# A 1-core two-block transformer kernel: all weight remainders and all vector work on VectorE, the 512-column products of a group ahead of its 256-column ones, and a new start-up sequence

## The chip, the cores and the metric

The kernel runs on one core of a Trainium2 chip. The metric is the device time of one execution in microseconds (us); the median of three executions before the change is 1955.4 us.

## What is computed

Two blocks, each of two layers, run one behind the other on one sequence of 256 tokens of width 1024, in float32. The reference, cut to what matters here:

```python
def hybrid_layer(x, p_i, ...):                       # first block, two layers
    proj = rmsnorm(x, g_pre_mix) @ w_in              # 3404 columns, split into q, k, v of A to D
    o_a = dsa_attention(rope(a_q), rope(a_k), a_v, rope(a_iq), rope(a_ik), iw)   # top 64 keys by an index score
    o_b = forgetting_attention(b_q, b_k, b_v, log_sigmoid(b_f + b_forget))
    o_c = differential_attention(rope(c_q), rope(c_k), c_v, lam, lam_init, diff_subln)
    o_d = sliding_window_sink_attention(rope(d_q), rope(d_k), d_v, sinks)
    x = x + rmsnorm(concat(o_a, o_b, o_c, o_d) @ w_out, g_post_mix)
    m = square(relu(rmsnorm(x, g_pre_mlp) @ w_up)) @ w_down
    x = x + rmsnorm(m, g_post_mlp)
    return x + sigmoid(x @ w_ple_gate) * (p_i @ w_ple_proj)

def second_block(x, ...):                            # two layers
    mix = hybrid_mixer(x, ...)                       # dilated window attention, retention, gates
    x = layer_norm(ALPHA * x + mix, ln1_g, ln1_b)
    x = layer_norm(ALPHA * x + swiglu(x, ...), ln2_g, ln2_b)
```

## The kernel before

**Products of split numbers.** Every large matmul is made of three products of parts. An operand is split into `hi`, a rounded copy, and `lo`, the rest that the rounding left. For weights, `Weights.load` (lines 91 to 121) brings a tile of up to 128x1024 numbers from HBM over SP's queue into `wraw` (4 buffers, line 98), copies it on ScalarE into `whi` (6 buffers, line 104) and subtracts into `wlo` (6 buffers, line 107). Which engine subtracts is taken from a list, `lo_engines` or `next`: VectorE mostly, GpSimd for 24 of the 628 tiles. These 24 are 11 in each layer of the first block (three in turn with VectorE, then all eight of the column groups 2120 and 1608 of `w_in`) and one in each layer of the second. Activations are split in the same way into `phl` (lines 232 and 233).

**The four kinds of product.** `mm_tok` (line 270) and `mm_pair` (line 286) hold the activation still and move 512 columns of weight. `mm_dim` (lines 315 to 317) moves 256 columns. `mm_wide` holds a 128x128 piece of weight still: the product with `whi` moves both parts of the activation, 512 columns (line 328), the product with `wlo` moves the `hi` part alone, 256 columns (line 329). It runs one group of eight such pairs for each block of 128 outputs, 2080 pairs in all, in the MLPs of the first block and in the projections and gated MLPs of the second.

**A layer of the first block.** `layer1` projects column groups of `w_in` in the order 768, 1280, 0, 512, 2120, 1608, 2380, 2892 (`proj`). The first two give the queries and keys of the index. `index` adds up scores (VectorE, line 526) and takes the best 64 by eight rounds of maximum and replacement (lines 532 and 533), then makes the mask (lines 536 and 537). Meanwhile TensorE runs the projections that follow, then attention A needs the mask: its first masked logits are written by VectorE at line 388, between the matmuls of lines 387, 412 and 420. While A's short matmuls wait for VectorE and ScalarE, TensorE fills the time with matmuls of group 1608. The bq and bk transposes (lines 372 and 363) come after that. After `w_out`, `norm(t)` scales and adds the residual in `xg` (line 805) and transposes it as input of the MLP, and `update(t)` (lines 813 and 814) brings X up to date on GpSimd.

**The second block** ends its first half with a layer norm, whose last operation is line 1056 and is followed by the transposes for the gated MLP. At that place GpSimd makes one `wlo` tile.

**The start.** `begin` (line 962) loads ident, positions, the rope frequencies and eight small constants over GpSimd's queue, x over SP's, and the first norm weight as two broadcasts to 128 partitions over ScalarE's queue. VectorE multiplies x by it (line 995) before the transposes. `setup1` computes the rope tables on VectorE and ScalarE, `scale` multiplies them by each token's norm, and the rope of the first projection (line 488) waits for them.

**What sets the order.** A scheduler orders the instructions of each engine from the program; an instruction passed to `pin` keeps its place in program order, and one passed to `behind` is issued after another one of its engine. So work that is moved to another engine changes the place of its neighbours too.

## Time and profile before

| | |
|---|---|
| median of three runs | 1955.4 us (1955.16 to 1962.62) |
| the profiled execution, its own time | 1958.0 us |
| its span | 1956.1 us |
| TensorE busy | 96% of the span |
| VectorE, ScalarE, GpSimd busy | 68%, 53%, 9% |
| mean granted TensorE clock | 0.988 of full speed |

The span reaches from the first to the last instruction of the profiled execution. A busy share counts an instruction from its start to its modelled end, so TensorE's 96% holds time in which a matmul waits its turn behind another one. Rows of the timeline carry, in brackets, how long the engine was idle before and what it waited for.

### The profile page before, as it was taken

The numbers are of one execution on the slowest core, as the hardware profiler recorded it, in microseconds if no ns is written. First come the engines' busy times: TensorE is split into PE (matmuls) and PEld (weight loads), VectorE is DVE, ScalarE is ACT, GpSimd is POOL, SyncE is SP. The second block draws the span as 40 slices with busy tenths as digits, with TensorE's granted clock in tenths as the row PEclk, the third lists the DMA queues.
The fourth block names the chain that finished last, engine by engine and source line by source line (L and its number), as shares of the span: only waits on it lengthen the run. The fifth ranks groups of instructions, "written<-read, shape, count | busy, mean of one in ns | idle before, by whom it ended". The sixth has DMA issues, their size and how long they took to land. (4 is left out here: it accounts for less than half of the span.)

```text
span 1956.1 us, 27859 instructions
## 1 busy us (share of the span) xinstructions
PE 1884.0 (96%) x10280; PEld 1614.1 (83%) x10280; DVE 1320.7 (68%) x2413; ACT 1044.4 (53%) x1751; POOL 166.4 (9%) x168
## 2 busy tenths in 40 slices
PE   6998999999989999999999999999999999999997
PEld 4786878878868888988888988888897888988886
DVE  6866756677677666758666677566668666677565
ACT  4555545465645445565555555554565555555552
POOL 3302100013030000000000000000000000000000
PEclk9998999999989999999999999999999999999999
DMA  6532576645326655645555756664554555656662
GB/s 190 154 118 83 184 236 206 201 138 162 117 73 206 201 174 165 194 147 181 159 178 178 227 174 204 181 199 147 163 171 151 179 179 171 206 168 205 191 192 89
DMA packets 187208, 334.52 MB, mean 171 GB/s; under 512 B 11548, under 2 KB 108882, under 8 KB 186688
## 3 DMA queue, kind: packets, MB, share of 16 engines
q1 hardware_dynamic: 180160, 308.94, 50.2%
q0 software_dynamic: 6624, 23.27, 3.8%
q8 instruction: 81, 1.33, 0.3%
q10 hardware_dynamic: 288, 0.52, 0.1%
q14 instruction: 55, 0.45, 0.1%
HBM read 331.62 MB, written 4.62 MB: 172 GB/s over the span
## 5 line engine op out<-in xcount | busy, mean ns | idle before, releaser
L107 DVE TENSOR_TENSOR wlo<-wraw,whi 128x1024 fp32r<-128x1024 f32 (+1 forms) x604 | 694.5, 1165 | 332.8 <-ACT whi L104 319.0
L104 ACT ACTIVATE whi<-wraw 128x1024 fp32r<-128x1024 f32 (+1 forms) x628 | 615.0, 998 | 370.1 <-PE bank L286 109.4
L328 PE MATMUL bank<-phl,whi 128*128 128x512 f32 x2080 | 740.1, 399 | 0.0
L329 PE MATMUL bank<-phl,wlo 128*128 128x256 f32 x2080 | 585.1, 281 | 0.7 <-DVE wlo L107 0.7
L328 PEld LDWEIGHTS bank<-phl,whi 128*128 128x128 f32 x2080 | 390.6, 188 | 92.8 <-DVE phl L233 0.6
L329 PEld LDWEIGHTS bank<-phl,wlo 128*128 128x128 f32 x2080 | 393.0, 189 | 3.9 <-DVE wlo L107 2.5
L286 PE MATMUL bank<-whi,phl 128*128 128x512 f32 x1280 | 360.0, 396 | 1.2 <-ACT phl L232 1.0
L270 PE MATMUL bank<-whi,phl 128*128 128x512 f32 (+4 forms) x1152 | 350.1, 384 | 6.1 <-ACT whi L104 4.1
L286 PEld LDWEIGHTS bank<-whi,phl 128*128 128x128 f32 x1280 | 237.9, 189 | 54.0 <-ACT phl L232 2.9
L270 PEld LDWEIGHTS bank<-whi,phl 128*128 128x128 f32 x1152 | 214.5, 194 | 38.0 <-ACT whi L104 5.2
L270 PE MATMUL bank<-wlo,phl 128*128 128x512 f32 (+4 forms) x576 | 216.3, 376 | 0.5 <-DVE wlo L107 0.5
L286 PE MATMUL bank<-wlo,phl 128*128 128x512 f32 x640 | 206.3, 394 | 0.1
L286 PEld LDWEIGHTS bank<-wlo,phl 128*128 128x128 f32 x640 | 120.5, 188 | 29.1 <-DVE wlo L107 2.4
L227 POOL TENSOR_TENSOR ry<-ry,mhalf 128x1 f32<-128x1 f32 (+1 forms) x40 | 33.0, 827 | 1152.8 <-DVE ry L226 1145.5
L270 PEld LDWEIGHTS bank<-wlo,phl 128*128 128x128 f32 x576 | 111.2, 193 | 16.0 <-DVE wlo L107 1.7
L317 PE MATMUL bank<-phl,wlo 128*128 128x256 f32 x304 | 86.5, 285 | 0.0
L316 PE MATMUL bank<-phl,whi 128*128 128x256 f32 x304 | 86.3, 284 | 0.0
L315 PE MATMUL bank<-phl,whi 128*128 128x256 f32 x304 | 85.5, 281 | 0.0
L232 ACT ACTIVATE phl<-bank 128x512 fp32r<-128x512 f32 (+2 forms) x64 | 35.3, 573 | 53.9 <-PE bank L251 53.2
L315 PEld LDWEIGHTS bank<-phl,whi 128*128 128x128 f32 x304 | 57.8, 190 | 0.6
L317 PEld LDWEIGHTS bank<-phl,wlo 128*128 128x128 f32 x304 | 57.6, 189 | 0.0
L233 DVE TENSOR_TENSOR phl<-bank,phl 128x512 fp32r<-128x512 f32 (+2 forms) x64 | 41.0, 661 | 24.5 <-ACT phl L232 24.4
(297 smaller groups left out, 1838.0 us busy)
## 6 DMA issues: line engine op xcount, KB each, us to landing
wraw<-in_w_in_dram SPq DMA_DIRECT2D x172, 512.0 KB, 4.5
wraw<-in_w_mlp_up_dram SPq DMA_DIRECT2D x64, 512.0 KB, 4.6
wraw<-in_w_mlp_down_dram SPq DMA_DIRECT2D x64, 512.0 KB, 4.5
wraw<-in_w_ffn_gate_dram SPq DMA_DIRECT2D x44, 512.0 KB, 4.6
wraw<-in_w_ffn_up_dram SPq DMA_DIRECT2D x44, 512.0 KB, 4.4
wraw<-in_w_ffn_down_dram SPq DMA_DIRECT2D x44, 512.0 KB, 4.5
wraw<-in_w_in_dram SPq DMA_DIRECT2D x54, 384.0 KB, 3.8
wraw<-in_w_out_dram SPq DMA_DIRECT2D x32, 512.0 KB, 3.8
```

Of the source, the lines that this page charges most:

```text
L104: nc.scalar.activation(hi[:, :n], src, AF.Copy)
L107: ins = eng.tensor_tensor(lo[:, :n], src, hi[:, :n].bitcast(F32), op=ALU.subtract)
L227: nc.gpsimd.tensor_tensor(y, y, self.mhalf[:, :n], op=ALU.pow)
L232: self.nc.scalar.activation(hi, src, AF.Copy)
L233: self.nc.vector.tensor_tensor(lo, src, hi.bitcast(F32), op=ALU.subtract)
L270: self.order(nc.tensor.matmul(ps, self.part(parts, kt)[x][:, sl], get(kt + kbase)[w], start=start and n == 0, stop=stop and n == len(terms ...
L286: ins = nc.tensor.matmul(pss[j], self.part(parts, kt)[x][:, sl], get(kt + kbase)[w][:, j * 512:(j + 1) * 512], start=start and n == 0, sto ...
L315: self.order(nc.tensor.matmul(ps, wh, xh, start=first, stop=False, **kw), n == 0)
L316: nc.tensor.matmul(ps, wh, xl, start=False, stop=False, **kw)
L317: nc.tensor.matmul(ps, wl, xh, start=False, stop=last, **kw)
L328: self.order(nc.tensor.matmul(flat, wh[:, c:c + P], both, start=n == 0, stop=False), n == 0)
L329: nc.tensor.matmul(ps[:, 0], wl[:, c:c + P], both[:, :S], start=False, stop=n == len(kts) - 1)
```

## The change

- `mm_wide` issues the eight 512-column products of a group first and the eight 256-column ones after them.
- The choice of an engine for `wlo` is gone: all 628 subtractions run on VectorE. The product of two norm weights (`gboth`), the two products `gain(t)` and the update of X, which GpSimd did, are on VectorE as well. The update reads PSUM itself, with the norm and the weight in one operation per half, so two ScalarE copies per token tile are gone; it is placed after `relu2(1)`.
- The start: the first norm weight is loaded as 8x128 numbers, transposed on TensorE into columns, and applied to the transposed x from PSUM. ident, norm weight, positions and frequencies come over ScalarE's queue. The first splits are pinned in order. The rope tables are made after x of both token tiles has been taken. The loads of the lambdas, masks and other constants stay on GpSimd's queue, behind `scale(1)`. The first projection runs on six of its eight pieces before it lets the other work in.

The core of the diff (line numbers of the changed file are 2 to 40 off those above):

```diff
@@ Weights.load
-            nc.scalar.activation(hi[:, :n], src, AF.Copy)
-            eng = self.next.pop(0) if self.next else self.lo_engines[self.n % len(self.lo_engines)]
-            self.n += 1
-            ins = eng.tensor_tensor(lo[:, :n], src, hi[:, :n].bitcast(F32), op=ALU.subtract)
+            first = nc.scalar.activation(hi[:, :n], src, AF.Copy)
+            ins = nc.vector.tensor_tensor(lo[:, :n], src, hi[:, :n].bitcast(F32), op=ALU.subtract)
@@ mm_wide
-            wh, wl = get(kt)
-            self.order(nc.tensor.matmul(flat, wh[:, c:c + P], both, start=n == 0, stop=False), n == 0)
-            nc.tensor.matmul(ps[:, 0], wl[:, c:c + P], both[:, :S], start=False, stop=n == len(kts) - 1)
+            self.order(nc.tensor.matmul(flat, get(kt)[0][:, c:c + P], both, start=n == 0, stop=False), n == 0)
+        for n, kt in enumerate(kts):
+            nc.tensor.matmul(ps[:, 0], get(kt)[1][:, c:c + P], self.part(parts, kt)[0], start=False,
+                             stop=n == len(kts) - 1)
@@ layer1
-            self.late.append(self.setup1)
-            self.late.append(lambda: scale(0))
+            self.late += [lambda: scale(0), lambda: scale(1), self.constants]
...
-        self.w.lo_engines = [nc.vector, nc.gpsimd]
         ps = proj(0, 512)
...
-        self.w.lo_engines = [nc.gpsimd]
         ps = proj(2120, 260)
...
-        nc.gpsimd.tensor_tensor(gboth, gboth, gmlp, op=ALU.mult)
+        self.pin(nc.vector.tensor_tensor(gboth, gboth, gmlp, op=ALU.mult))
...
-            nc.gpsimd.tensor_tensor(o, X[t], gmlp, op=ALU.mult)
+            nc.vector.tensor_tensor(o, X[t], gmlp, op=ALU.mult)
...
-                self.pin(nc.scalar.activation(u[:, sl], pss[t][j], AF.Copy, scale=r))
-            us[t] = u
-            self.pin(nc.gpsimd.tensor_tensor(us[t], us[t], gpost, op=ALU.mult))
-            nc.gpsimd.tensor_tensor(X[t], X[t], us[t], op=ALU.add)
+                self.pin(nc.vector.scalar_tensor_tensor(u[:, sl], pss[t][j], rs[t], gpost[:, sl], op0=ALU.mult,
+                                                        op1=ALU.mult))
+            self.pin(nc.vector.tensor_tensor(X[t], X[t], u, op=ALU.add))
@@ begin
-        nc.gpsimd.dma_start(self.ident, self.a["ident"])
...
-            nc.scalar.dma_start(g[:, sl], self.a["norm_pre_mix"][0, sl].partition_broadcast(P))
+        nc.scalar.dma_start(self.ident, self.a["ident"])
+        nc.scalar.dma_start(gr, self.a["norm_pre_mix"][0].rearrange("(k p) -> k p", p=P))
...
+        self.late += [lambda: load(1), lambda: take(1, 0), lambda: take(1, 1), self.setup1, second, lambda: squares(0),
+                      lambda: squares(1)]
@@ second block, gated MLP
-                self.w.next = [nc.vector] * 3 + [nc.gpsimd]
```

**How the order moves, 1: the remainders of groups 2120 and 1608.** GpSimd before, in the first layer, from the end of group 512 on (the numbers behind the names tell buffers apart; 780 and 260 columns are group 2120, 1024 are two pieces of group 1608):

```order
L107 TENSOR_TENSOR wlo_733<-wraw_730,whi_732 128x780
L107 TENSOR_TENSOR wlo_739<-wraw_736,whi_738 128x780
L107 TENSOR_TENSOR wlo_745<-wraw_742,whi_744 128x260
L107 TENSOR_TENSOR wlo_751<-wraw_748,whi_750 128x260
L107 TENSOR_TENSOR wlo_894<-wraw_891,whi_893 128x1024
L107 TENSOR_TENSOR wlo_900<-wraw_897,whi_899 128x1024
L107 TENSOR_TENSOR wlo_906<-wraw_903,whi_905 128x1024
L107 TENSOR_TENSOR wlo_912<-wraw_909,whi_911 128x1024
```

VectorE after the change, same layer, the end of the top-64 search, the mask, and later the first tiles of group 1608:

```order
L529 MAX top_664<-score_502 128x8
L103 TENSOR_TENSOR wlo_749<-wraw_746,whi_748 128x260
L530 MATCH_REPLACE score_502<-top_664,score_502 128x256
L103 TENSOR_TENSOR wlo_755<-wraw_752,whi_754 128x260
L533 TENSOR_SCALAR score_494<-score_494 128x128
...
L387 ISA pr_790,mx_789<-bank_791,score_494 128x128
...
L487 TENSOR_TENSOR rope_890<-bank_806,cr32_284 128x8x16
L103 TENSOR_TENSOR wlo_898<-wraw_895,whi_897 128x1024
...
L103 TENSOR_TENSOR wlo_904<-wraw_901,whi_903 128x1024
```

The last remainders of group 2120 stand at the end of the search, and the first of group 1608 stands 24 instructions behind the first masked logits, where GpSimd made it during the search.

**2: TensorE at the same place.** Before, the matmuls of group 1608 (line 270) ahead of the first of the two logits matmuls that wait for the mask (line 387):

```order
L270 MATMUL bank_915<-whi_893,phl_132 128x512
L270 MATMUL bank_915<-wlo_894,phl_132 128x512
L270 MATMUL bank_915<-whi_893,phl_132 128x512
L270 MATMUL bank_915<-wlo_894,phl_132 128x512
L270 MATMUL bank_915<-whi_893,phl_132 128x512 x2
L270 MATMUL bank_915<-whi_899,phl_132 128x512
L387 MATMUL bank_787<-kT_609,qT_610 128x128
L270 MATMUL bank_915<-whi_899,phl_132 128x512
```

After the change:

```order
L386 MATMUL bank_796<-kT_613,qT_614 128x128
L411 MATMUL bank_819<-ident_79,pr_790 128x128 x4
L419 MATMUL bank_838<-v_730,pt_824 128x64 x4
L386 MATMUL bank_850<-kT_613,qT_624 128x256
L386 MATMUL bank_855<-kT_613,qT_624 128x256
L268 MATMUL bank_919<-wlo_898,phl_114 128x512
L268 MATMUL bank_919<-whi_897,phl_114 128x512
```

Attention A's first token tile (lines 386, 411 and 419) now runs with no matmul of group 1608 between, and the stream of that group begins with `wlo_898`.

**3: GpSimd's queue at the start.** Before and after, from the DMA of the frequencies or the norm's powers on:

```order
L212 DMA c_freq_109<-const_freq_dram 128x48
L979 DMA lq_115<-in_lambda_q1_dram 128x2x32
...
L212 DMA c_causal_122<-const_causal_dram 128x256
...
L227 TENSOR_TENSOR ry_263<-ry_263,mhalf_80 128x1
L227 TENSOR_TENSOR ry_276<-ry_276,mhalf_80 128x1
```

```order
L225 TENSOR_TENSOR ry_262<-ry_262,mhalf_80 128x1
L225 TENSOR_TENSOR ry_275<-ry_275,mhalf_80 128x1
L976 DMA lq_286<-in_lambda_q1_dram 128x2x32
...
L976 DMA c_causal_287<-const_causal_dram 128x256
```

The lambdas and masks were issued ahead of the norm's powers, and are issued behind them.

## Rows read from the trace of the kernel before

**Rows 1.** The page, part 1: busy us, share of the span, instructions of each engine.

```profile
PE 1884.0 (96%) x10280; PEld 1614.1 (83%) x10280; DVE 1320.7 (68%) x2413; ACT 1044.4 (53%) x1751; POOL 166.4 (9%) x168
```

**Rows 2.** TensorE's waits: operation, waited for, us in total, times, longest.

```profile
PE bank L251 <- DVE x L1056: 6.0, 3, 2.2
PE bank L251 <- DVE xg L805: 4.9, 4, 2.2
...
PE bank L329 <- DVE wlo L107: 0.7, 3, 0.4
```

**Rows 3.** Windows: a stretch's busy us (and instructions) by engine, granted clock, DMA, GB/s.

```profile
197.40:200.80 3.40, 3.40 (x10) 2.66 (x9) 3.29 (x3) 2.30 (x4) 2.12 (x2) 0.51 0.30 36
```

**Rows 4.** DMA, 0 to 30 us: rates in 40 slices of 0.75 us; one issue.

```profile
GB/s 0 0 49 221 218 167 287 374 320 356 374 268 55 96 147 186 148 156 169 146 177 332 381 336 317 341 264 275 330 340 280 318 181 195 401 104 112 330 265 131
...
lq<-in_lambda_q_dram POOLq DMA_DIRECT2D x2, 32.0 KB, 7.8
```

**Rows 5.** Timeline of VectorE, first layer: x of token tile 1, first rope.

```profile
23.33 1.29 DVE L995 TENSOR_TENSOR xg<-x,row 128x512 f32<-128x512 f32 x2
...
40.39 0.68 DVE L488 TENSOR_TENSOR w<-bank,cr 128x512 f32<-128x512 f32 x1
```

**Rows 6.** Timeline of GpSimd, first layer, its remainders.

```profile
58.72 4.49 POOL L107 TENSOR_TENSOR wlo<-wraw,whi 128x780 fp32r<-128x780 f32 x3 [10.23 <-ACT whi L104]
...
77.46 4.71 POOL L107 TENSOR_TENSOR wlo<-wraw,whi 128x1024 fp32r<-128x1024 f32 x2 [1.68 <-PE bank L270]
```

**Rows 7.** Timeline of VectorE, first layer: scores, mask, first masked logits.

```profile
60.75 3.74 DVE L526 SCALAR_TENSOR_TENSOR score<-rl,iw,score 128x128 f32<-128x128 f32 x3
...
64.75 0.72 DVE L526 SCALAR_TENSOR_TENSOR score<-rl,iw,score 128x128 f32<-128x128 f32 x2
...
80.27 2.05 DVE L537 TENSOR_TENSOR score<-score,c_causal 128x128 f32<-128x128 f32 x1
...
82.48 0.29 DVE L388 CUSTOM_DVE_ANT_0 pr<-bank,score 128x128 f32<-128x128 f32 x1
```

**Rows 8.** Timeline of TensorE, first layer: the wait for the mask, the bq transposes.

```profile
82.83 0.49 PE L387 MATMUL bank<-kT,qT 128*128 128x128 f32 x2 [3.07 <-DVE mx L388]
...
99.52 0.39 PE L372 MATMUL bank<-ident,bq 128*128 128x128 f32 x2
```

**Rows 9.** Timeline of VectorE, second layer: the scores.

```profile
442.85 4.44 DVE L526 SCALAR_TENSOR_TENSOR score<-rl,iw,score 128x128 f32<-128x128 f32 x4 [2.11 <-ACT rl L523]
```

**Rows 10.** Timelines of VectorE and GpSimd, first layer: `norm` of both token tiles, update.

```profile
170.11 1.42 DVE L805 SCALAR_TENSOR_TENSOR xg<-u,ry,xg 128x512 f32<-128x512 f32 x2 [0.67 <-POOL ry L227]
...
190.42 5.64 DVE L805 SCALAR_TENSOR_TENSOR xg<-u,ry,xg 128x512 f32<-128x512 f32 x2 [0.67 <-POOL ry L227]
...
190.37 2.39 POOL L813 TENSOR_TENSOR u<-u,row 128x1024 f32<-128x1024 f32 x1
```

**Rows 11.** Timelines of VectorE and GpSimd, second block: the first layer norm.

```profile
1172.45 3.52 DVE L1056 SCALAR_TENSOR_TENSOR x<-x,ry,row 128x512 f32<-128x512 f32 x2
...
1172.28 2.49 POOL L107 TENSOR_TENSOR wlo<-wraw,whi 128x1024 fp32r<-128x1024 f32 x1
```

**Rows 12.** Timeline of TensorE: a group of `mm_wide`, then 512-column and 256-column runs.

```profile
209.69 0.40 PE L328 MATMUL bank<-phl,whi 128*128 128x512 f32 x1
...
212.53 0.40 PE L328 MATMUL bank<-phl,whi 128*128 128x512 f32 x1
...
1170.91 0.62 PE L286 MATMUL bank<-whi,phl 128*128 128x512 f32 x2
...
1172.95 0.61 PE L286 MATMUL bank<-whi,phl 128*128 128x512 f32 x2
...
961.85 0.28 PE L315 MATMUL bank<-phl,whi 128*128 128x256 f32 x1
...
963.65 0.28 PE L315 MATMUL bank<-phl,whi 128*128 128x256 f32 x1
```

**Rows 13.** The page, part 5: VectorE's remainders, busy us and mean ns of one.

```profile
L107 DVE TENSOR_TENSOR wlo<-wraw,whi 128x1024 fp32r<-128x1024 f32 (+1 forms) x604 | 694.5, 1165 | 332.8 <-ACT whi L104 319.0
```

140 lines of the change are left out of this document (87 added, 53 removed).

## The prediction

> **What bounds the kernel now.** I read the page's busy shares first, then TensorE's waits, then the timelines around each long wait. TensorE is busy 96% of the span, VectorE 68%, GpSimd 9% [rows 1]. So an instruction put on VectorE costs time only where TensorE waits for VectorE, and what can be won lies in TensorE's waits and in how fast its matmuls follow each other. The table of waits names few places, and several end at a VectorE operation that took far too long. The operation of line 805 took 1.42 us for two in one place and 5.64 us for two of the same shape in another; in the second, GpSimd ran a 128x1024 product from 190.37 us on [rows 10]. The same holds for line 1056: 3.52 us for two, with GpSimd at a `wlo` tile [rows 11]; for three scores in 3.74 us, where two took 0.72 us after GpSimd had ended [rows 6, 7]; for the mask, 2.05 us at 80.27 us, while GpSimd had a `wlo` pair from 77.46 us for 4.71 us [rows 6, 7]; and for four scores of the second layer in 4.44 us [rows 9]. After such a wait the granted clock stands at 0.51 for 3.4 us [rows 3], which is the lower of the two levels (1.2 instead of 2.4 GHz): half of that stretch, 1.7 us, is lost.
>
> **The start and the first layer's mask (A).** Before, x of token tile 1 was multiplied at 23.33 us and the first rope began at 40.39 us [rows 5]. The transfers moved 290 to 370 GB/s from 4.5 to 8 us and over 300 again from 16 us on, but 55 to 190 GB/s from 9 to 16 us, the 13th to the 21st slice, while the small constants of GpSimd's queue were landing (a lambda takes 7.8 us) [rows 4]. Now the two broadcasts of 256 KB are 4 KB in all, and the constants come later. Ahead of the end of x there are 3.0 MB (two x tiles of 0.5 MB, four weight tiles of 0.5 MB). At 350 GB/s that is 8.6 us, counted from 4.5 us on: about 13.5 us, and 1 us for the transposes that now come first. From x to rope it was 40.39 - 23.33 = 17.1 us; GpSimd made two `wlo` tiles in it, and I take each to have stretched one operation of VectorE by 2.1 us, between the 1.7 us of the mask (2.05 us against the 0.36 us of a score of the same shape) and the 2.7 us of the three scores (3.74 us against 1.08) [rows 7]; the two tiles come to VectorE, 2 x 1.17 us [rows 13]. 13.5 + 1 + 17.1 - 4.2 + 2.3 = 29.7, so **the rope begins at about 30 us**, 10 us earlier. The bounds are 28 us (if nothing else is late) and 34 us (if ScalarE's chain of splits, squares and sine sets it).
>
> From rope to the first masked logits at 82.48 us it was 42.1 us [rows 7]. In it the stretched operations go: 2.7 us of the three scores and 1.7 us of the mask, and for what GpSimd's other tiles in that stretch do to VectorE an estimated 3.1 us, in the same proportion: 7.5 us in all. VectorE takes over one tile of 1024 columns, two of 780 and two of 260 before that point: 1.17 x 3104 / 1024 = 3.5 us. So 42.1 falls to 38.1 us, and the logits come at about 68 us, 14.4 us earlier.
>
> Behind them some of this is paid back. GpSimd made the four tiles of group 1608 during the search, so TensorE had matmuls of that group ready as filling between attention A's short ones. By the order now, VectorE makes the first of these tiles 24 instructions after the first masked logits. The stretch from there to the bq transposes was 99.52 - 82.48 = 17.0 us [rows 7, 8]. About 20 of group 1608's 48 matmuls of 0.227 us [rows 12] were done as filling in the first 6.5 us, 4.5 us of work that is now behind; part of it fills later gaps, so the price is 2.5 to 5 us, and I take 3.7. TensorE also sits idle longer ahead of it (it was 3.07 us, [rows 8]), so one more stretch at half clock, 1 to 2 us. **A = -14.4 + 3.7 + 1.7 = -9 us**, between -14 and -4.
>
> **The second layer's mask (B).** There is no start there. The stretched operations go (-7.5, the scores' 4.44 us [rows 9] among them), 3.5 us of tiles come, the filling is lost (+3.7) and the clock falls (+1). **B = +1 us**, between -2 and +4.
>
> **The update (C).** TensorE waits 4.9 us for line 805, in four places [rows 2], of which the second token tile of each layer has nearly all. Without GpSimd's update those two operations take 1.42 us and end before TensorE has finished the matmuls ahead. The stall of some 2.3 us and half of a stretch at half clock, 1.7 us, go in each of two layers, 8 us. The update on VectorE (two operations of 512 columns at 0.71 us as in [rows 10] and a sum of 1024 at 1.17 us as in [rows 13], 2.6 us for each token tile) now lies in the first MLP products; VectorE has room there, but I keep back 1.5 us. **C = -6.5 us**, between -8.5 and -4. The ScalarE copies that fall away were hidden (ScalarE is at 53%, [rows 1]): 0. `gboth` and `gain` on VectorE, some 1.2 us each, delay `wlo` tiles of `w_out` that are made ahead: 0, with 1 us either way.
>
> **The layer norm of the second block (D).** TensorE waits 6.0 us for line 1056 in three places [rows 2]; two have a GpSimd `wlo` beside them, about 2 us each, the third has none and stays. With 1.7 us of clock each that is 7.4 us. VectorE gets 1.2 us for the tile, just there: **D = -6 us**, between -7.5 and -4.
>
> **Wide products first (E).** A group of eight pairs takes 212.53 - 209.69 = 2.84 us. Nine 512-column matmuls in a row took 2.04 us, 0.227 each; fifteen of 256 columns 1.80 us, 0.120 each [rows 12]. Eight of each would be 2.77 us, 0.07 less, or 17 us over the 260 groups. Against it: in the pairs, with a narrow one at 0.120, a wide one takes 0.355 - 0.120 = 0.235 us; if that is its own price, whatever comes behind it, the order gives nothing, and with 2 ns more for each narrow one it costs 2080 x 0.002 = 4 us. The 512-column runs hold the activation and move weights, where `mm_wide` holds weights, so they are near but not the same; I take a third of the 17 us, **E = -6 us**, between -17 and +4. The narrow products need `wlo` later than before, but TensorE waited for it only 0.7 us [rows 2], so that adds nothing.
>
> **Sum.** -9 + 1 - 6.5 - 6 - 6 = -26.5 us. It stands against the profiled execution's own time, 1958.0 us, which gives 1931.5 us. The median of the runs shown is 2.6 us lower, so the forecast is **1929 us**.
>
> **The rivals.**
> - *The order of products is worth nothing* (E = 0): 1935 us. For it speaks the 0.235 us of a wide matmul in the pairs; against it the 0.227 us of the other runs [rows 12]. The Trainium skill, "TensorE: Matmul & The Clock Gate", "Wait — 56ns, not 53.3ns?", has back-to-back matmuls start N / 2.4 GHz plus about 2.5 ns apart, with no term for the order of sizes; by that rule both orders cost the same, and this would be the outcome. The trace's 0.227 us for 512 columns lies above the rule's 0.216 us, so something else has a share in it. Chance 0.11.
> - *The late tiles of group 1608 cost more*: if all filling is lost and the clock falls twice, A is -4 and B +4: 1937 us. For it speaks that four tiles now wait behind attention A's work on VectorE; against it that TensorE waited only 3.07 us there. Chance 0.13.
> - *The constants come too late*: the lambdas go out behind the norm's powers. VectorE's first operation on them, and the work queued behind it up to the mask, would wait; with 8 us to land [rows 4] this is close, and I price it at 5 us: 1934 us. The Trainium skill, "SBUF — State Buffer", "SBUF: two separate sides", warns that a DMA issued from GpSimd's queue has its descriptors held up while VectorE copies in its two-port modes. By that rule the new place, amid the rope tables' copies, is worse than the old one; no row here shows it. Chance 0.08.
> - *VectorE becomes the bound in the first block, and the kernel is slower.* Each layer puts about 11 us of `wlo` and 9 us of products and updates on VectorE. If nearly all of that showed at the mask and at `norm`, where TensorE already waits for it, 40 us come on, of which 9 are in the sum above, and a stretch at half clock behind each of four new waits, 7 us: 1929 + 31 + 7 = 1967 us. It decides from about two thirds of the added work on: below that the kernel stays faster. Against it: 68% busy [rows 1], 0.7 us of waits for `wlo` [rows 2]. Chance 0.06.
>
> **How the numbers follow.** The forecast has 0.62. All good ends of the terms give 1906 us, all bad ends 1951 us; they won't fall together, so 8 in 10 is 1912 to 1948 us, which holds the first three rivals. Half a per cent, 9.8 us, is about what a measurement of this kernel can tell from no change: faster means under 1945.6 us, slower over 1965.2 us. Faster has the forecast and the first three rivals but for their slow ends, 0.82; the slow ends and the mild part of the last rival are no change, 0.12; slower has 0.06.
>
> **What would show it.** Right: the first rope at about 30 us; first masked logits at about 68 us, with group 1608's first matmul after, and 20 us from there to the bq transposes; lines 805 and 1056 at 1.4 us for two everywhere, no wait and no half clock behind the second token tile; a group of wide products at 2.80 us or less. Wrong: a VectorE operation over 2 us with GpSimd idle; VectorE waiting for a lambda; a wait for `wlo` in the MLPs; a rope that starts after 34 us.

## The result, and the profile after

The changed kernel takes 1937.7 us (median of four executions, 1934.9 to 1940.2), beside 1956.3 us of the kernel before in the same comparison: a ratio of 0.9898, 95% interval 0.9872 to 0.9924. That is 18.6 us faster by the medians. The profiled execution took 1937.2 us, its span is 1935.4 us, 20.7 us under that of before. The forecast was 1929 us, 26.5 us faster by its sum. It was right that the change wins, mostly by the stated mechanisms, and it promised too much; the time lies on the rival in which the late tiles of group 1608 cost more.

The page of the changed kernel, part 1 (busy us, share of the span, instructions) and part 5 (a group; busy us, mean ns of one; idle time before, and what ended most of it):

```profile
PE 1877.3 (97%) x10282; PEld 1614.0 (83%) x10282; DVE 1306.8 (68%) x2456; ACT 1035.9 (54%) x1743; POOL 77.8 (4%) x127
...
L103 DVE TENSOR_TENSOR wlo<-wraw,whi 128x1024 fp32r<-128x1024 f32 (+1 forms) x628 | 711.0, 1147 | 328.7 <-ACT whi L102 238.6
```

VectorE took over 24 tiles, the updates and the products, and is busy 1306.8 us, 13.9 us *less* than before [rows 1]. GpSimd is busy 88.6 us less. Small parts of the start fell away too, but the main reason is that VectorE's operations are no longer stretched beside GpSimd: the groups that were stretched fell by about 36 us together (line 805 of before from 14.4 to 6.0 us, the index scores from 17.1 to 11.6), and the work taken over added about 32.

The times at which TensorE reaches certain places (timelines of TensorE; us from the start of the span) show where the 20.7 us come from:

| place | before | after | difference |
|---|---|---|---|
| first rope transposes | 43.07 | 32.27 | -10.8 |
| products for the index scores | 50.75 | 39.41 | -11.3 |
| A's first products with v, layer 1 | 87.44 | 74.92 | -12.5 |
| bq transposes, layer 1 | 99.52 | 94.07 | -5.45 |
| first wide product, MLP of layer 1 | 204.11 | 195.02 | -9.1 |
| first rope transposes, layer 2 | 420.37 | 409.82 | -10.55 |
| A's first products with v, layer 2 | 471.66 | 455.48 | -16.2 |
| bq transposes, layer 2 | 483.21 | 474.10 | -9.1 |
| first wide product, MLP of layer 2 | 587.93 | 573.94 | -14.0 |
| first wide product of the second block | 796.95 | 780.86 | -16.1 |
| ahead of the first layer norm, behind it | 1151.61, 1201.68 | 1135.20, 1183.65 | -16.4, -18.0 |
| ahead of the second, behind it | 1732.96, 1782.80 | 1714.36, 1762.76 | -18.6, -20.0 |
| last matmul | 1945.66 | 1925.20 | -20.5 |

Read down the last column: the start wins 11 us early, and in each layer of the first block 7.07 us are handed back between A's first products with v and the bq transposes. TensorE's waits of the changed kernel (operation, waited for, us in total, times, longest):

```profile
PE bank L419 <- ACT pt L413: 7.0, 12, 1.2
...
PE bank L411 <- ACT pr L398: 5.8, 4, 1.6
PE bank L249 <- DVE x L1093: 4.5, 3, 2.2
...
PE bank L268 <- DVE wlo L103: 2.3, 2, 1.8
```

The 4.9 us of waits for `norm` (then line 805) [rows 2] are gone. The layer norm still has 4.5 us in three places, from 6.0 [rows 2]. The waits of short attention matmuls for ScalarE (`pt`, `pr`) grew by 4.8 us; group 1608 used to fill more of that time. In the kernel before they were:

```profile
PE bank L420 <- ACT pt L414: 5.2, 10, 0.7
...
PE bank L412 <- ACT pr L399: 2.8, 4, 1.1
```

The granted clock in stretches of the changed kernel (windows; the column before the last two is the clock):

```profile
40.60:44.00 3.40, 3.40 (x10) 2.66 (x9) 0.45 (x2) 0.73 (x2) 0.00 (x0) 0.50 1.01 361
74.70:81.50 6.80, 6.58 (x20) 5.57 (x21) 3.85 (x12) 2.27 (x4) 0.00 (x0) 0.50 0.28 81
453.60:460.40 6.80, 6.11 (x19) 4.76 (x20) 3.98 (x13) 2.05 (x8) 0.00 (x0) 0.50 0.26 77
1167.00:1172.00 5.00, 3.78 (x19) 2.60 (x19) 3.46 (x6) 1.60 (x3) 1.63 (x3) 1.00 0.65 198
1354.70:1358.10 3.40, 3.37 (x12) 3.40 (x13) 1.74 (x3) 1.52 (x3) 0.00 (x0) 0.50 0.00 0
```

and of the kernel before:

```profile
43.80:47.20 3.40, 3.40 (x15) 3.16 (x14) 2.48 (x10) 2.85 (x5) 1.11 (x1) 0.51 0.00 0
467.20:470.50 3.30, 3.30 (x11) 2.46 (x10) 3.27 (x16) 2.03 (x12) 0.00 (x0) 0.50 1.02 401
```

Attention A now runs 6.8 us at the lower level (1.2 GHz) in each layer, which costs 3.4 us. Before, it did so for 3.4 us in layer 2 and not at all in layer 1, so 3.4 us of the loss are new in layer 1 and 1.7 us in layer 2. The first layer norm's stretch is now at full clock; the second layer of that block has a new one of 3.4 us at the lower level (1354.7 us), behind its layer norm. VectorE and ScalarE of the changed kernel in the first layer (timelines; in brackets the idle time before and what ended it):

```profile
16.74 0.69 DVE L1011 TENSOR_TENSOR xg<-bank,cols 128x512 f32<-128x512 f32 x1 [0.86 <-PE bank L1006]
...
29.68 0.68 DVE L485 TENSOR_TENSOR w<-bank,cr 128x512 f32<-128x512 f32 x1
...
35.82 1.06 ACT L102 ACTIVATE whi<-wraw 128x1024 fp32r<-128x1024 f32 x1 [3.83 <-DMA wraw<-in_w_in_dram]
...
37.80 0.19 DVE L462 SCALAR_TENSOR_TENSOR lscr<-lq 128x32 f32<-128x32 f32 x1 [1.22 <-DMA lq<-in_lambda_k_dram]
...
67.93 0.41 DVE L103 TENSOR_TENSOR wlo<-wraw,whi 128x260 fp32r<-128x260 f32 x1
...
69.87 0.28 DVE L387 CUSTOM_DVE_ANT_0 pr<-bank,score 128x128 f32<-128x128 f32 x1
...
73.85 1.21 DVE L103 TENSOR_TENSOR wlo<-wraw,whi 128x1024 fp32r<-128x1024 f32 x1
```

The first rope stands at 29.7 us, where it was 40.4 [rows 5]; the first masked logits at 69.9 us, where they were 82.5 [rows 7]. The `whi` of the last tile of group 2120 was ready at 53.1 us, and VectorE made the last `wlo` of that group 15 us later, at the end of the search. TensorE at the same places:

```profile
39.41 1.23 PE L517 MATMUL bank<-ikT,iqT 128*128 128x128 f32 x6 [3.27 <-ACT ikT L363]
...
72.25 1.48 PE L411 MATMUL bank<-ident,pr 128*128 128x128 f32 x4 [1.32 <-ACT pr L398]
...
74.92 1.97 PE L419 MATMUL bank<-v,pt 128*128 128x64 f32 x8 [1.19 <-ACT pt L413]
...
78.14 0.99 PE L268 MATMUL bank<-wlo,phl 128*128 128x512 f32 x1
...
94.07 0.38 PE L371 MATMUL bank<-ident,bq 128*128 128x128 f32 x2
```

No matmul of group 1608 comes ahead of 78 us, and A's matmuls wait 1.2 to 1.3 us at a time for ScalarE with nothing to fill in.

### The profile page after: what moved, and what is told of

The parts are those of the page before. It is cut to its first block, busy times and chain, and to the rows that moved or that the text cites. A ratio compares the mean times of both kernels' runs of the same rounds, so it can differ in the third digit from the quotient of the medians.

```text
span 1935.4 us, 27780 instructions
## 1 busy us (share of the span) xinstructions
PE 1877.3 (97%) x10282; PEld 1614.0 (83%) x10282; DVE 1306.8 (68%) x2456; ACT 1035.9 (54%) x1743; POOL 77.8 (4%) x127
## 4 chain that ended last, share of the span: by engine, by line
PE 83%; DVE 7%; DMA 4%; ACT 4%; issue 2%; POOL 0%; DVEq 0%; SPq 0%; ACTq 0%; POOLq 0%
PE bank L325 23%; PE bank L284 20%; PE bank L268 13%; PE bank L327 12%; DMA wraw<-in_w_in_dram 3%; DVE wlo L103 2%; PE bank L386 2%; PE bank L419 2%; PE bank L315 2%; PE bank L314 2%; PE bank L313 2%; ACT whi L102 1%; PE bank L249 1%; ACT pr L398 1%; PE bank L411 1%
## 5 line engine op out<-in xcount | busy, mean ns | idle before, releaser
L103 DVE TENSOR_TENSOR wlo<-wraw,whi 128x1024 fp32r<-128x1024 f32 (+1 forms) x628 | 711.0, 1147 | 328.7 <-ACT whi L102 238.6
L102 ACT ACTIVATE whi<-wraw 128x1024 fp32r<-128x1024 f32 (+1 forms) x628 | 608.9, 997 | 346.1 <-PE bank L284 110.2
L325 PE MATMUL bank<-phl,whi 128*128 128x512 f32 x2080 | 532.3, 395 | 0.4 <-ACT whi L102 0.4
L325 PEld LDWEIGHTS bank<-phl,whi 128*128 128x128 f32 x2080 | 374.9, 189 | 69.1 <-ACT whi L102 1.2
L268 PE MATMUL bank<-whi,phl 128*128 128x512 f32 (+4 forms) x1152 | 341.2, 378 | 4.3 <-ACT whi L102 2.2
L327 PEld LDWEIGHTS bank<-phl,wlo 128*128 128x128 f32 x2080 | 284.2, 190 | 23.2 <-DVE wlo L103 2.7
L327 PE MATMUL bank<-phl,wlo 128*128 128x256 f32 x2080 | 291.8, 283 | 0.6 <-DVE wlo L103 0.6
L315 PE MATMUL bank<-phl,wlo 128*128 128x256 f32 x304 | 86.3, 284 | 0.0
L313 PEld LDWEIGHTS bank<-phl,whi 128*128 128x128 f32 x304 | 57.7, 190 | 0.2
L314 PEld LDWEIGHTS bank<-phl,whi 128*128 128x128 f32 x304 | 57.3, 189 | 0.2
L315 PEld LDWEIGHTS bank<-phl,wlo 128*128 128x128 f32 x304 | 57.5, 189 | 0.0
```

The lines of the kernel that those rows point to most:

```text
L102: first = nc.scalar.activation(hi[:, :n], src, AF.Copy)
L103: ins = nc.vector.tensor_tensor(lo[:, :n], src, hi[:, :n].bitcast(F32), op=ALU.subtract)
L268: self.order(nc.tensor.matmul(ps, self.part(parts, kt)[x][:, sl], get(kt + kbase)[w], start=start and n == 0, stop=stop and n == len(terms ...
L313: self.order(nc.tensor.matmul(ps, wh, xh, start=first, stop=False, **kw), n == 0)
L314: nc.tensor.matmul(ps, wh, xl, start=False, stop=False, **kw)
L315: nc.tensor.matmul(ps, wl, xh, start=False, stop=last, **kw)
```

## The experiments

Two theories were set against each other for the 7.07 us: the *place* of VectorE's late tiles in the order (they could have been made earlier), or VectorE's *time* (the work itself is too much there). Others took one part of the change back, or took away one suspected cost. All ratios are to the kernel before on the same chip.

**1. The pairs again (`e1_pairs`).**

```diff
             self.order(nc.tensor.matmul(flat, get(kt)[0][:, c:c + P], both, start=n == 0, stop=False), n == 0)
-        for n, kt in enumerate(kts):
             nc.tensor.matmul(ps[:, 0], get(kt)[1][:, c:c + P], self.part(parts, kt)[0], start=False,
```

> The changed kernel with the products of mm_wide in pairs again, 512 columns then 256. Theory (the order of products gains by the pace of the matmuls alone): a group of eight pairs goes back from about 2.79 to 2.82 us, so the MLPs and projections that use it are 4 to 6 us longer in all, 1942 us, and every other stage stays within 1 us. Rival (the order gains nothing; what the MLP stages gained came from VectorE's or ScalarE's waits): the time stays within 1 us of 1937 us and the pairs take the same 2.80 us.

Measured: 1940.8 us, 0.9911 (0.9894 to 0.9927). By the ratios that is 2.5 us more, and the intervals overlap, so the times alone don't settle it. The timelines of TensorE show the groups themselves, first with the pairs:

```profile
217.59 0.40 PE L325 MATMUL bank<-phl,whi 128*128 128x512 f32 x1
...
220.42 0.40 PE L325 MATMUL bank<-phl,whi 128*128 128x512 f32 x1
```

and in the changed kernel:

```profile
220.85 2.00 PE L325 MATMUL bank<-phl,whi 128*128 128x512 f32 x8
222.69 1.11 PE L327 MATMUL bank<-phl,wlo 128*128 128x256 f32 x8
223.65 2.00 PE L325 MATMUL bank<-phl,whi 128*128 128x512 f32 x8
```

Eight pairs take 220.42 - 217.59 = 2.83 us; eight wide and eight narrow ones take 223.65 - 220.85 = 2.80 us. Of that the wide ones have 222.69 - 220.85 = 1.84 us, 0.230 us each, and the narrow ones 0.120 us each. Over the groups (some 180 of the 260) with no other matmul between, the mean is 2.82 us in pairs, here and in the kernel before, and 2.79 us in the new order. So the order is worth 0.025 us a group, 6.5 us if all 260 gained it. Between the places of the table above, the stages that use `mm_wide` are 4.3 us longer here and the others 0.7 us shorter.

**2. The remainders of groups 2120 and 1608 on GpSimd again (`e2_gpsimd_lo`).**

```diff
+        self.w.eng = nc.gpsimd
         ps = proj(2120, 260)
...
+        self.w.eng = nc.vector
         ps = proj(2380, 512)
```

> The changed kernel with the remainders of groups 2120 and 1608 on GpSimd again (8 of the 11 tiles in each first-block layer), all else on VectorE. Theory (the 7 us that each layer pays between the first masked logits and the bq transposes come from these remainders being late in VectorE's order): that stretch falls from 24.2 us to about 17 us, as in the kernel before, while the operations of the mask and scores stretch again and the masked logits come 2 to 4 us later; net 3 to 5 us a layer, 1928 to 1931 us. Rival (VectorE is simply short of time there, so that what is taken off it comes back as stretched operations): the stretch shortens by less than 3 us or the logits come later by as much; 1935 to 1940 us.

Measured: 1934.5 us, 0.9873 (0.9856 to 0.9889), not to be told apart from the changed kernel. VectorE and GpSimd of this kernel (timelines):

```profile
49.55 5.58 POOL L104 TENSOR_TENSOR wlo<-wraw,whi 128x780 fp32r<-128x780 f32 x4 [13.63 <-DVE wlo L104]
49.80 6.12 DVE L524 SCALAR_TENSOR_TENSOR score<-rl,iw,score 128x128 f32<-128x128 f32 x5
...
66.35 0.61 DVE L530 MAX8 top<-score 128x8 f32<-128x256 f32 x2
...
67.53 0.61 DVE L530 MAX8 top<-score 128x8 f32<-128x256 f32 x2
...
70.25 4.79 POOL L104 TENSOR_TENSOR wlo<-wraw,whi 128x1024 fp32r<-128x1024 f32 x2 [1.74 <-PE bank L269]
70.73 2.11 DVE L535 TENSOR_TENSOR score<-score,c_causal 128x128 f32<-128x128 f32 x1
72.76 2.42 DVE L534 TENSOR_SCALAR score<-score 128x256 f32<-128x256 f32 x1
75.11 0.28 DVE L388 CUSTOM_DVE_ANT_0 pr<-bank,score 128x128 f32<-128x128 f32 x1
```

Five scores take 6.12 us, the mask 4.5 us, all beside GpSimd, and the masked logits come at 75.1 us instead of 69.9. But the filling is back: from there to the bq transposes (92.79 us) it is 17.7 us, where the changed kernel needs 94.07 - 69.87 = 24.2 and the kernel before needed 17.0 [rows 7, 8]. So moving these tiles to VectorE won 5.2 us ahead of the logits and lost 6.5 us behind them. Neither theory's sum is met; both halves are seen.

**3. The same tiles on VectorE, but earlier in the program (`e3_preload`).** Loads and splits of group 2120 are written ahead of the matmuls of group 512, and half of those of group 1608 ahead of group 2120's.

```diff
-        ps = proj(512, 256)
+        g512 = self.w.cols(w_in, 512, 256)
+        g2120 = self.w.cols(w_in, 2120, 260)
+        ps = proj(512, 256, g512)
...
-        ps = proj(2120, 260)
+        h1608 = self.w.load(w_in, 0, 4, 1608, 512)
+        ps = proj(2120, 260, g2120)
...
-        ps = proj(1608, 512)
+        r1608 = self.w.load(w_in, 4, 4, 1608, 512)
+        ps = proj(1608, 512, lambda kt: (h1608 if kt < 4 else r1608)(kt))
```

> The changed kernel with the loads and splits of group 2120 written ahead of the matmuls of group 512, and those of the first half of group 1608 ahead of the matmuls of group 2120, so that VectorE makes these remainders before or during the search and not after it; no work added or removed. Theory (late place in the order, not lack of time): the wait for wlo of 1.8 us before the mask goes, the masked logits come 2 to 3 us later for two more tiles of 1.2 us, and the stretch behind them falls from 24 to 18 to 20 us; net 3 to 4 us a layer, 1929 to 1932 us. Rival (VectorE is short of time): the masked logits come as much later as the stretch shortens, 1936 to 1939 us.

Measured: 1925.8 us, 0.9831 (0.9815 to 0.9847), 13 us under the changed kernel by the ratios, and outside its interval. VectorE and TensorE of this kernel (timelines):

```profile
71.91 0.28 DVE L387 CUSTOM_DVE_ANT_0 pr<-bank,score 128x128 f32<-128x128 f32 x1
...
89.04 0.39 PE L371 MATMUL bank<-ident,bq 128*128 128x128 f32 x2
```

The work on VectorE is the same (1305.8 us busy); the logits even come 2.0 us later, as the tiles now stand in front of them. The stretch behind them is 17.1 us, where the kernel before had 17.0. So the place was the cost, not the time. The edit moves loads and ScalarE's copies too; experiment 9, which leaves them where they are, shows that this isn't needed for the gain. The gain is larger than was expected.

**4. The lambdas later still (`e4_lambda_late`).** The four lambda loads wait until the end of the search, and their use is put behind group 1608.

```diff
-            for j, nm in enumerate(("lambda_q1", "lambda_k1", "lambda_q2", "lambda_k2")):
-                q(self.lq[:, :, j, :], self.a[nm].partition_broadcast(P))
...
+            self.pin(nc.vector.memset(self.lq, 0.0))
+            for j, nm in enumerate(("lambda_q1", "lambda_k1", "lambda_q2", "lambda_k2")):
+                q(self.lq[:, :, j, :], self.a[nm].partition_broadcast(P))
...
+        if i == 0:
+            self.lambdas()
```

> The changed kernel with the four loads of the lambdas moved from the place behind the norm's powers to one behind the score search (a memset of their tile on VectorE holds them back), and VectorE's work on them behind the bq transposes. Theory (the lambda's small packets of 1 to 2 us each slow the weight tiles between 28 and 36 us, so that ScalarE waits 3.8 us for a weight tile and TensorE 3.4 us for ScalarE): the wait of TensorE at 36 us and the half clock behind it go, the masked logits come 3 to 5 us earlier, 1932 to 1934 us, unless the packets then slow group 1608's tiles instead. Rival (the tile is late because its buffer came free late, not because of the packets): the wait at 36 us stays, and the time is within 2 us of 1937 us.

Measured: 1934.3 us, 0.9878 (0.9863 to 0.9893): no difference that these runs can tell. TensorE's wait of 3.3 us ahead of the index scores falls to 0.9 us, the half clock there is gone, and the logits come at 66.2 us, 3.7 earlier. Then the lambdas go out at 66 to 68 us, a weight tile of group 1608 issued at 72.1 us takes 10.1 us to land, and the bq transposes stand at 94.38 us, as in the changed kernel. A norm weight loaded there is slow as well; it took 7.3 us in the changed kernel, where it is issued at 38 us (DMA issues, 60 to 90 us; KB, median us from issue to landing):

```profile
row<-in_norm_post_mix_dram POOLq DMA_DIRECT2D x1, 512.0 KB, 10.6
```

The lambdas took their harm along. Their 128 KB are 64 packets of 2 KB, and the trace holds how long each took: 1.6 us on average here, 6.2 us of all 16 DMA engines together between 67.8 and 76.0 us, where a weight tile's packets of the same size take 0.08 us each. But they aren't alone: the two norm weights of 512 KB that the queue issues right behind them take another 2.5 us of all engines. The reading has a second limit: in this kernel the last `wlo` tiles of group 2120 also stand earlier on VectorE, so a part of the 3.7 us is theirs.

**5. The update and one `wlo` tile of the second block on GpSimd again (`e5_update_back`).**

```diff
-                self.pin(nc.vector.scalar_tensor_tensor(u[:, sl], pss[t][j], rs[t], gpost[:, sl], op0=ALU.mult,
-                                                        op1=ALU.mult))
-            self.pin(nc.vector.tensor_tensor(X[t], X[t], u, op=ALU.add))
+                self.pin(nc.scalar.activation(u[:, sl], pss[t][j], AF.Copy, scale=rs[t]))
+            self.pin(nc.gpsimd.tensor_tensor(u, u, gpost, op=ALU.mult))
+            nc.gpsimd.tensor_tensor(X[t], X[t], u, op=ALU.add)
...
+                self.w.next = [nc.vector] * 3 + [nc.gpsimd]
```

> The changed kernel with two pieces of work on GpSimd again, in places far apart: the update of X in the first block (with its ScalarE copies), and one wlo tile at the layer norm of the second block. Theory (GpSimd's operations block those of VectorE that run beside them): line 805's pair for the second token tile takes over 5 us again, TensorE waits 2.3 us more with 1.7 us of half clock in each first-block layer, 7 to 8 us in all; the layer norm's pair takes 3.5 us again, with 2.05 us of wait for the first token tile and half clock, while the new 1.3 us wait of the second token tile goes, so 2 to 3 us more for each second-block layer. In all 11 to 14 us over the changed kernel, 1949 to 1951 us. Rival (the gain at norm came from the update's later place alone, and the layer norm's from something else): the pairs take 1.4 us beside GpSimd, and the time is within 3 us of 1937 us.

Measured: 1946.0 us, 0.993 (0.9916 to 0.9945): by the ratios 6.3 us over the changed kernel, where 11 to 14 were expected. The span is 8.7 us longer, +3.7 and +3.85 at the MLPs' entries and +1.55 and +1.7 at the layer norms; some 2 us of these 10.8 are got back between them. VectorE and GpSimd of this kernel (timelines):

```profile
193.84 4.84 DVE L104 TENSOR_TENSOR wlo<-wraw,whi 128x1024 fp32r<-128x1024 f32 x2 [1.25 <-ACT whi L102]
194.33 3.26 POOL L813 TENSOR_TENSOR x<-x,u 128x1024 f32<-128x1024 f32 x1
...
1162.30 3.53 DVE L1094 SCALAR_TENSOR_TENSOR x<-x,ry,row 128x512 f32<-128x512 f32 x2
```

A pair of `wlo` tiles takes 4.84 us where two take 2.3 (1147 ns each in part 5 above), beside GpSimd's sum; TensorE then waits 1.77 us for a `wlo`, with 3.4 us at half clock behind. The layer norm's pair takes 3.53 us again, as expected. Line 805's pair for the second token tile stays at 1.42 us, against the expectation: the update runs here from 191.8 us on, behind that pair, where it ran beside it in the kernel before. So GpSimd stretches what runs beside it, and what it hits depends on when it runs. At `norm` itself this run doesn't part GpSimd from the update's later place.

**6. The old start with all the rest (`e6_old_start`).** `begin`, `setup1` and the late list of the first layer are those of the kernel before; one piece of it:

```diff
-            self.late += [lambda: scale(0), lambda: scale(1), self.constants]
+            self.late.append(self.setup1)
+            self.late.append(lambda: scale(0))
```

> The changed kernel with the start of the kernel before (norm weight by broadcast, constants first, rope tables in the old place), all else changed. Theory (the start is worth what the first rope shows, 10.7 us, less the 3.4 us wait and the half clock that the lambdas now cause at 36 us): first rope at about 38 us, since the two stretched table operations are gone with GpSimd's tiles, masked logits at about 76 us against 69.9 us, and 5 to 7 us over the changed kernel, 1943 to 1945 us. Rival (the first layer is bound by VectorE's total work up to the mask, whatever the start): logits within 2 us of 69.9 us, and 1937 to 1939 us.

Measured: 1941.6 us, 0.9907 (0.9893 to 0.9922), by the ratios 1.8 us over the changed kernel, with intervals that overlap. The first rope stands at 40.53 us, no earlier than before [rows 5] and 2.5 us later than expected, though no GpSimd tile runs beside VectorE in this kernel. Of the 10.8 us by which the new start brings the rope forward, 4.85 are left at the bq transposes; what reaches the end these times can't tell.

The edit does more than it was meant to. GpSimd's queue, with no tiles to make, now issues the two norm weights of 512 KB at 26.4 and 27.0 us (82.1 and 82.7 us before), and a weight tile issued at 27.6 us lands after 8.0 us (3.9 us for the tile of that place before). ScalarE waits for it, and its sine, without which there is no rope, comes at 38.1 us:

```profile
35.77 1.06 ACT L102 ACTIVATE whi<-wraw 128x1024 fp32r<-128x1024 f32 x1 [2.96 <-DMA wraw<-in_w_in_dram]
```

So another wait took the place of the stretched operations, and this run doesn't show the old start alone.

**7. The kernel before, with its lambdas on one partition (`e7_before_narrow`).** The 32 KB broadcasts become 256 bytes each; the finished factor is spread over the partitions by one small matmul with ones.

```diff
-            nc.gpsimd.dma_start(self.lq[:, :, j, :], self.a[nm].partition_broadcast(P))
+            nc.gpsimd.dma_start(self.lq[:1, :, j, :], self.a[nm].rearrange("(o d) e -> o d e", o=1))
...
+        nc.tensor.matmul(ps[:, :DEPTH], one, row, start=True, stop=True)
+        nc.vector.tensor_copy(neglam, ps[:, :DEPTH])
```

> The kernel before with one change: the four lambda loads write one partition instead of 128 (the factor is then spread by a matmul with ones). Theory (the lambdas' small packets slowed the weight tiles between 9 and 16 us): the rate there stays above 250 GB/s, the first projection's tiles land 3 to 5 us earlier, the first rope begins 2 to 5 us earlier than 40.4 us, and the end follows by 2 to 5 us, 1952 to 1955 us against about 1957 us. Rival (the 0.5 MB of broadcast norm weight and the other constants are what takes the rate): the rate between 9 and 16 us stays under 200 GB/s and nothing moves.

Measured: 1954.7 us (ten executions), 0.9973 (0.9964 to 0.9983). The DMA rates of this kernel, 0 to 30 us in 40 slices of 0.75 us:

```profile
GB/s 0 0 52 172 248 167 276 377 328 353 373 372 372 287 350 404 399 406 320 225 223 358 374 385 373 322 358 202 90 128 371 205 128 355 180 0 60 202 385 74
```

The hole of 55 to 190 GB/s between 9 and 16 us [rows 4] is gone: 287 to 406 GB/s in the 13th to 18th slices. The first rope comes at 35.3 instead of 40.4 us, 3.9 us are left at the bq transposes and about 5 at the end (0.27%, 3.3 to 7 by the interval).

**8. Experiments 3 and 7 together, on the changed kernel (`e8_both`).** The edits are those shown.

> The changed kernel with the early remainders of the run e3 and with the lambdas loaded to one partition. Theory: the wait of TensorE at 36 us (3.4 us and half clock) goes, no slow packets come later either, and it adds to what e3 gained: masked logits 3 to 5 us earlier than in e3, 1921 to 1923 us. Rival (the tile at 36 us is late for another reason, or what is won before the mask is paid back behind it): within 2 us of e3, 1924 to 1927 us.

Measured: 1924.8 us, 0.9823 (0.9809 to 0.9838), not to be told from experiment 3. The logits come 3.5 us earlier (68.4 us) and the bq transposes 3.1 (85.9 us), and the later attention gives it back, at least in part, in two stretches at half clock that are longer than in experiment 3 (10.2 us each, from 159.6 and 535.0 us, where they were 6.8).

**9. In group 1608, all products with `whi` ahead of those with `wlo` (`e9_hi_first`).** Splits and loads are those of the changed kernel; only TensorE's order within the group differs.

```diff
         terms = self.terms(kts, start)
+        if lo_last:
+            terms.sort(key=lambda m: m[2])
...
-        ps = proj(1608, 512)
+        ps = proj(1608, 512, lo_last=True)
```

> The changed kernel with one change in group 1608: its products with whi all come before those with wlo, for each token tile, as mm_wide does now; nothing else moved. Theory (the loss behind the mask is TensorE waiting for late wlo tiles while the whi tiles are there): about 16 matmuls can run ahead of or between attention A's, but only for the two whi tiles whose raw buffers are free, so half of the 7 us of each layer comes back, 3 us a layer, 1930 to 1933 us. Rival (without the raw buffers nothing more can be filled in, since the loads of the second half still start only when VectorE frees a buffer): 1935 to 1938 us.

Measured: 1924.4 us, 0.9833 (0.9818 to 0.9848), as far down as experiment 3 and more than was expected. TensorE of this kernel (timeline):

```profile
71.41 0.86 PE L270 MATMUL bank<-whi,phl 128*128 128x512 f32 x3
...
90.53 0.39 PE L373 MATMUL bank<-ident,bq 128*128 128x128 f32 x2
```

TensorE finds matmuls of group 1608 at 71.41 us that need only `whi`, 78.14 - 71.41 = 6.7 us before the changed kernel's first one. The stretch from the logits (71.57 us) to the bq transposes is 19.0 us instead of 24.2; the first MLP begins at 189.8 instead of 195.0 us, the second at 561.3 instead of 573.9. The loads of the second half of group 1608 are issued at 70 us here too, so it isn't the raw buffers that the late tiles hold which cost the time: it is TensorE standing behind a product whose `wlo` is late.

**10. Experiments 3, 7 and 9 together (`e10_all`).** The edits are those shown.

> The kernel of e8 (early remainders, lambdas on one partition) with group 1608's whi products ahead of its wlo products. Theory: the waits for wlo of 2.9 us in the first layer and 1.6 us in the second, and the half clock behind the first, go, since 16 to 20 matmuls are ready without wlo: 4 to 6 us under e8, 1919 to 1921 us. Rival (TensorE then only waits for the mask itself, which VectorE sets): within 2 us of e8, 1923 to 1926 us.

Measured: 1920.0 us (1917.4 to 1920.3), 0.9805 (0.9788 to 0.9821): 37 us under the kernel before, and 0.9% under the changed one, the fastest version here. Its span is 1918.5 us. No half clock is left in the first layer ahead of 153 us. Its longest wait (operation, waited for, us in total, times, longest):

```profile
PE bank L249 <- DVE mix L584: 6.8, 2, 3.4
```

Its interval touches those of experiments 8 and 9, so how much each of the parts adds to the others is not settled. What is left is this wait of the transposes of `mix`, ahead of `norm`, the attention's short matmuls (5.1 us for `pt`), and the layer norms (4.7 us).

## Why the prediction was right or wrong

| term | forecast | measured between | measured |
|---|---|---|---|
| A, start and first mask | -9 | begin to bq, layer 1 | -5.45 |
| B, second mask | +1 | first rope to bq, layer 2 | +1.4 |
| C, update | -6.5 | bq to first wide product, both layers | -3.6 - 4.9 = -8.5 |
| D, layer norm of block 2 | -6 | around both layer norms | -1.6 - 1.4 = -3.0 |
| E, order of products | -6 | first block's MLPs, rest of block 2 | -1.5 - 2.1 - 1.3 = -4.9 |
| sum | -26.5 | | -20.5 |

The rows of the table overlap somewhat (C's stretch holds the rest of the attention too), but they add up to the difference at the last matmul. Of the 6 us between forecast and measured, A missed 3.55, D 3.0, E 1.1 and B 0.4; C gave 2.0 more than forecast.

**A, the start: right by errors that cancel.** The rope was forecast at 29.7 us and stands at 29.68. But x of token tile 1 is first taken at 16.74 us, not at 14.5 (4.5 and 8.6 make 13.1 and not 13.5, and behind 16 us the rates were over 300 GB/s without a break only to 19.5 [rows 4]). From x to rope it then takes 12.9 us, not 15.2; where these 2.3 us come from isn't shown. The step "I take each to have stretched one operation of VectorE by 2.1 us" was right in size. The two operations in the kernel before (timeline of VectorE), beside GpSimd's tiles at 32.04 and 36.53 us:

```profile
32.16 2.35 DVE L442 TENSOR_SCALAR turns<-ang 128x96 f32<-128x96 f32 x1
...
36.56 2.51 DVE L453 COPY cs<-sincos 128x32 f32<-128x32 f32 x2
```

They take 0.21 and 0.41 us in the changed kernel. Not all of it lay on the way to the rope: behind the first, ScalarE's sine waited only 0.49 us for VectorE; the second stood directly ahead of the rope.

**A, from the rope to the logits: nearly right, 69.9 us and not 68.** Missing was the place to which the lambdas went. They now land at 32 to 38 us, their packets take 5.3 us of all DMA engines in that time, and the weight tile that the index products need comes late: ScalarE waits 3.83 us for it, TensorE 3.27 us for ScalarE, and a stretch of 3.4 us at half clock follows. That clock is no new loss: the kernel before had as long a one at 43.8 us, behind its wait of 3.84 us at the first rope transposes. The rival "the constants come too late" had this place, but the wrong victim: VectorE itself waits only 1.22 us for a lambda; it is the transfer beside them that suffers.

**A and B, the payback: right in kind, too small.** "I take 3.7" and "one more stretch at half clock, 1 to 2 us" made 5.4 us; the stretch grew from 17.0 to 24.2 us, 7.2 us, of which 3.4 are the clock. The estimate counted the lost filling, and one short stall's clock; it overlooked that TensorE, with nothing to fill in, stays at the lower level for 6.8 us. (Of group 1608's matmuls the timeline of before has 15 to 17 in the 6.5 us behind the first logits, and seven ahead of them, so "about 20" took in some of the latter.) Experiments 3 and 9 show that all or most of this was to be had back without taking any work from VectorE. In B the gain ahead was larger than thought, 16.2 - 10.55 = 5.65 us where -7.5 and +3.5 made 4, and the payback was again 7.07 us where 4.7 were forecast, only 1.7 of it by the clock here; the sum, +1.4, was met all the same.

**C: right.** Line 805 takes 1.42 us for two at both token tiles, and TensorE's wait for it is gone. VectorE in the changed kernel:

```profile
185.52 1.42 DVE L802 SCALAR_TENSOR_TENSOR xg<-u,ry,xg 128x512 f32<-128x512 f32 x2 [0.68 <-POOL ry L225]
...
1156.05 1.41 DVE L1093 SCALAR_TENSOR_TENSOR x<-x,ry,row 128x512 f32<-128x512 f32 x2
...
1160.16 3.48 DVE L103 TENSOR_TENSOR wlo<-wraw,whi 128x1024 fp32r<-128x1024 f32 x3
...
1167.70 1.41 DVE L1093 SCALAR_TENSOR_TENSOR x<-x,ry,row 128x512 f32<-128x512 f32 x2
```

The 1.5 us held back for VectorE's new work were not needed: the update fits in the MLP. A part of layer 2's 4.9 us isn't `norm`'s: the half clock ahead of its `w_out` lasts 6.8 us, where it lasted 10.2. That the stretch at `norm` came from GpSimd rests on [rows 10], where the same pair took 1.42 us without it; experiment 5 shows GpSimd's cost at the MLPs' entries (+7.55 us), but through the `wlo` tiles, and so leaves open what the later place alone would have done.

**D: half of it, because the next late thing was not named.** The stretched 3.52 us [rows 11] are 1.41 us, and the half clock is gone; that clock, 1.7 us, is about all that the first layer gained. The wait did not shrink: it was 1.89 us and is now 0.71 us for ScalarE's `phl` and 1.16 us for the second token tile. "VectorE gets 1.2 us for the tile, just there" should have asked what else stands in that row (and counted it for both layers): three `wlo` tiles in a run, 3.48 us, where there had been two, now lie ahead of the second token tile's norm, and its transposes wait (TensorE, changed kernel):

```profile
1168.59 1.29 PE L249 MATMUL bank<-ident,x 128*128 128x128 f32 x8 [1.16 <-DVE x L1093]
```

That no longer stands behind GpSimd, but behind VectorE's own order. A kernel with the norm ahead of the third tile was not tried.

**E: right in size by the pace of the groups; at the end the two times can't be told apart (experiment 1).** The row of 0.227 us for 512 columns was a fair guide: the wide products take 0.230 us in the new order. Narrow ones take 0.120 us, as in the rows of 256 columns. The row "rest of block 2" also holds the new half clock at 1354.7 us; without its 1.7 us the term would be -6.6. The Trainium skill, "TensorE: Matmul & The Clock Gate", "Wait — 56ns, not 53.3ns?", has starts N / 2.4 GHz plus about 2.5 ns apart, with no term for what stands next to a matmul; by that rule both orders would cost the same. The groups don't bear that out: 2.79 against 2.82 us.

**The rivals.** *The late tiles of group 1608 cost more* came nearest in time (1937 us) and in mechanism, though B was not +4 and D made the rest. *Order worth nothing* fell with the pace of the groups in experiment 1. *VectorE becomes the bound* fell: it is less busy than before, and all the waits for `wlo` come to 2.9 us (0.6 of them at line 327). The rule on DMAs from GpSimd's queue (the Trainium skill, "SBUF — State Buffer", "SBUF: two separate sides") would have the lambdas land later now, as they are issued at 26 to 29 us, while VectorE makes the rope tables. DMA issues of the changed kernel, 0 to 45 us:

```profile
lq<-in_lambda_k_dram POOLq DMA_DIRECT2D x2, 32.0 KB, 8.6
```

The others are `lambda_q`, 6.9 us. Before, they took 7.8 us (`lambda_q`) [rows 4] and 9.6 us (`lambda_k`), so this trace doesn't show it.

## What to carry to other kernels

When work moves to an engine that executes in order, ask not only whether that engine has time, but behind which instructions the work will stand, and which stream of another engine begins with its result; experiments 3 and 9 gained 13 us without moving any work between engines, by making the late operand earlier or by using it later. A second engine whose operations stretch those of the first is worth less than its busy share: the 88.6 us of GpSimd's work that went away left VectorE less busy, not more. And a gain at the start is only as good as what follows it: of 10.8 us at the rope 4.85 were left at the bq transposes (experiment 6). A run that takes one cost away can let another in at the same place, as experiment 6 did: look at what the freed queue does next before calling the first cost hidden.

## What was not expected of the hardware

- **Small broadcasts hold up large loads.** Four lambdas of 32 KB, written as short pieces on 128 partitions, pull the rate of all queues down to 55 to 190 GB/s while they land; on one partition the same stretch moves 287 to 406 GB/s (experiment 7). Of their 64 packets of 2 KB, 37 to 47 took over 1 us in the three kernels looked at (before, changed, experiment 4), where a weight tile's 2 KB take 0.08 us. Moving them in time moved most of the harm (experiment 4).
- **VectorE's search runs freely beside GpSimd.** In experiment 2 the rounds of MAX8 and MATCH_REPLACE8 keep their step of 1.18 us (66.35 to 67.53 us) while GpSimd is at a `wlo` pair from 63.75 us for 4.77 us; scores and masks, of the kinds SCALAR_TENSOR_TENSOR, TENSOR_TENSOR and TENSOR_SCALAR, are held until about the end of GpSimd's instruction: the mask's two operations (0.3 to 0.4 us become 2.1 and 2.4) end at 72.84 and 75.18 us, and GpSimd's two tiles, 2.4 us each from 70.25 us on, at about 72.65 and 75.04.
- **Work on GpSimd also holds up what its queue loads.** The two norm weights of 512 KB go out at 82 us before, behind GpSimd's tiles, and at 36 and 38 us in the changed kernel. Where they go out amid the first weight tiles, they slow them (experiment 6).
- **A row of short matmuls without filling costs in the clock as well as in waits.** In the first layer TensorE waits 1.3 and 1.2 us between attention A's matmuls, and the granted clock is 0.50 for 6.8 us there; the kernel before had none. In the second layer it was 3.4 us before and is 6.8 us now. With the filling back (experiments 3 and 9) 3.4 us are left in the first layer and none in the second.
